# Splitting a layer's weights by DMA: a rounding load for the first part, an accumulating load for the second, both from GpSimd

## The chip, the cores and the metric

The kernel runs on one core of a Trainium2 chip. The metric is device time in microseconds (us) of one execution. The engines are named as in the profile: PE (TensorE matmul), PEld (its weight loads), DVE (VectorE), ACT (ScalarE), POOL (GpSimd) and SP (SyncE, which issues DMAs). An engine's name with a q (SPq, POOLq) is its instruction queue.

## What is computed

One decoder layer in float32 on 512 tokens of width 1024: a token mixer (an SSD group and a retention group behind one input projection), cross attention into 256 memory tokens, and a gated feed-forward with a short convolution, each followed by a layer norm.

```python
mix = _mixer(x, w_in, ..., w_mix_out, ...)      # projections 1024 -> 5648, SSD, retention, 2048 -> 1024
x = _layer_norm(ALPHA * x + mix, ln1_g, ln1_b)
xa = _memory_cross_attention(x, mem, w_xq, w_xk, w_xv, w_xo)
x = _layer_norm(ALPHA * x + xa, ln2_g, ln2_b)
ff = _conv_glu_ffn(x, w_ffn_up, b_ffn_up, ffn_conv_w, ffn_conv_b, w_ffn_down)
x = _layer_norm(ALPHA * x + ff, ln3_g, ln3_b)
```

## The kernel before

All dense products run in float32r, a rounded float32 that PE takes at full rate. To keep float32's precision each operand is split in two float32r parts: a first part h, the operand rounded, and a second part l, what the rounding left. A product is then three matmuls (`mm3`: h by h, h by l, l by h).

The weights come as one stream of 157 groups of [128, 1024] float32 (512 KB each), in the order in which PE uses them; below they are numbered 0 to 156. `Stream.push` fetches the next group and splits it: SP issues a DMA into a raw buffer (line 124), ACT rounds it into `wh` (line 126, a cast), and DVE, or GpSimd for the twelve groups in `POOL_L`, subtracts to get `wl` (line 128). `Stream.get` hands out one group and pushes up to three groups ahead of it: `wh` and `wl` have four buffers each (`RING`), the raw buffers are three (`RAW`). A buffer of `wh` and `wl` is free for group n when PE has finished group n-4.

Groups 0 to 15 are the projections to q, k and v of the retention, 16 to 27 those that feed the convolution, with the retention core woven between, 28 to 43 the two gates, with the SSD core woven between, 44 to 59 the mixer's output projection, 60 to 75 the memory's keys and values, 76 to 91 the attention's query and output projections, and 92 to 156 the feed-forward. A full group is 24 matmuls of 512 columns; for the keys and values it is half as much work. Three places hold four groups at once: the last groups of attention (88 to 91), the first four of the feed-forward (92 to 95, function `halves`), and the very last four (153 to 156, function `last`).

PE's order is the order of writing (`pin`). On the other engines, each of which takes its own instructions in order, a scheduler sets the order. GpSimd's own work is spread over the layer: rotary and SSD products, the reciprocal roots of the norms (lines 257 and 258), and a dozen plain loads of 512 KB that it issues itself: rows of norm weights (line 253), a mask (line 370) and the residual (line 642).

Of the kernel before, what the change touches and what calls it, by code (L numbers as in the profile page):

```python
# [7 lines left out]
F32 = mybir.dt.float32  # L8
# [5 lines left out]
P = 128  # L14
# [15 lines left out]
WARM = 9  # L30
# weight groups whose second part GpSimd takes
POOL_L = set(range(60, 68)) | set(range(92, 96))
RAW = 3
NS = 20

# columns of the constant array
C_ID, C_TRI, C_STR, C_ONE = 0, 128, 256, 384
# [9 lines left out]
C_W = C_SELJ + 4  # L47
# columns of the parameter array
P_CONV, P_GNW, P_GNB, P_FF = 0, 60, 68, 76
# [4 lines left out]
def tile_layer(ctx, tc, wst, wdt, xt, xn, memt, rows, small_row, par, cst, mdec, out):  # L54
    nc = tc.nc
# [3 lines left out]
    ring = ctx.enter_context(tc.tile_pool(name="ring", bufs=RING))  # L59
# [7 lines left out]
    def nm(s):  # L67
        uid[0] += 1
        return f"{s}_{uid[0]}"
# [16 lines left out]
    mult, add, sub = ALU.mult, ALU.add, ALU.subtract  # L86
    tt, stt, ts = nc.vector.tensor_tensor, nc.vector.scalar_tensor_tensor, nc.vector.tensor_scalar
    gtt = nc.gpsimd.tensor_tensor

    def f(t):  # L90
        return t.bitcast(F32)

    # The tensor engine runs its instructions in the order in which they are written here.
    last_pe = [None]
# [14 lines left out]

# [1 line left out]
    class Stream:  # L111
# [6 lines left out]
        def push(self, parts=1, between=None):  # L118
            r = ring.tile([P, 1024], F32, tag="raw", name=nm("raw"), bufs=RAW)
            h = ring.tile([P, 1024], F32R, tag="wh", name=nm("wh"))  # L120
            l = ring.tile([P, 1024], F32R, tag="wl", name=nm("wl"))
            for i in range(parts):
                c = slice(i * 1024 // parts, (i + 1) * 1024 // parts)
                nc.sync.dma_start(out=r[:, c], in_=wst[self.n][:, c])  # L124
                copy = nc.vector.tensor_copy if parts > 1 and i == 0 else nc.scalar.copy
                copy(out=h[:, c], in_=r[:, c])  # L126
                sub_l = gtt if self.n in POOL_L else tt
                sub_l(out=l[:, c], in0=r[:, c], in1=f(h[:, c]), op=sub)  # L128
                if between is not None:
                    between(i, copy)  # L130
            self.q.append((h, l))
            self.n += 1
# [9 lines left out]

    # The tensor engine's clock rises only once it works: it turns over while the first loads are on
    # their way.
    idle = t2(mybir.dt.bfloat16)
# [8 lines left out]

# [1 line left out]
    def mm3(o, a, b, start, stop):  # L156
# [45 lines left out]

# [1 line left out]
    xT = [slot("x", [P, 4, T], F32R) for _ in range(4)]  # L204
# [8 lines left out]
    for j in range(4):  # L213
        r = big([P, 1024])
        rv = r.rearrange("p (k t) -> p k t", k=2)
        xv = xt[j].rearrange("p (k t) -> p k t", k=2)
        h = xT[j // 2][:, 2 * (j % 2):2 * (j % 2) + 2, :]
        l = xT[2 + j // 2][:, 2 * (j % 2):2 * (j % 2) + 2, :]
# [19 lines left out]
    ones = cs[:, C_ONE:C_ONE + P]  # L238
# [26 lines left out]

# [1 line left out]
    QK = [big([P, 2, 512]) for _ in range(NT)]  # L267
# [23 lines left out]

# [1 line left out]
    wdr = cpool.tile([P, KD, 2, 16], F32R, name="wdr")  # L293
# [3 lines left out]
    dt = cpool.tile([P, 64], F32, name="dt")  # L297
# [10 lines left out]
    def dt_chain():  # L308
# [25 lines left out]
        for j in (13, 11, 9, 7, 5, 3, 1):  # L334
# [7 lines left out]
            in0=av.rearrange("p (q j) -> p q j", q=16).unsqueeze(2).to_broadcast([P, 16, 8, 4]),  # L342
            in1=sgn.unsqueeze(1).unsqueeze(3).to_broadcast([P, 16, 8, 4]), op=mult)
# [4 lines left out]
        nc.scalar.activation(out=ev, in_=b[:, :192].rearrange("p (j x) -> p j x", j=3), func=AF.Exp)  # L348
        # The differences of the running sums between two positions come from the tensor engine.
        # Four heads take 32 rows: the sums in two parts against ones, and ones against minus the sums.  # L350
        b = bank()
# [12 lines left out]
    dense = seq(tok(x_lhs, all8, NT, rotary(1)), *[tok(x_lhs, all8, NT, v_done(n)) for n in range(2)])  # L364
    weave(dt_chain(), dense)
    drain(dense)

# [1 line left out]
    maskdec = slot("row", [P, 8, P], F32, 2)  # L369
# [76 lines left out]

# [1 line left out]
    BT = big([P, 2, T])  # L448
# [51 lines left out]
    dense = xbc()  # L500
    weave(retention(), dense)
    drain(dense)

# [1 line left out]
    norm_w = bcast_row(rows[0:1, :])  # L505
# [14 lines left out]
    def ssd():  # L520
# [4 lines left out]
        for c in range(NT):  # L525
# [10 lines left out]
            cb = t2()  # L536
# [4 lines left out]
            def seg(q):  # L541
                g = q // 2
                b = bank()
                r = slice(32 * q, 32 * q + 32)
                mmul(b, seg_w[0][r, 1, tk], sr[r, :])
                # at or before a position the difference is at most 0; the others fall to cb's mask
                es[q] = t2()
                nc.scalar.activation(out=es[q], in_=b, func=AF.Relu, scale=-1.0)
                nc.scalar.activation(out=es[q], in_=es[q], func=AF.Exp, scale=-1.0)
                tt(out=hv(es[q], 4), in0=hv(es[q], 4),  # L550
                   in1=cb[:, g * P:(g + 1) * P].unsqueeze(1).to_broadcast([P, 4, P]), op=mult)
# [46 lines left out]

# [1 line left out]
    def twice_silu(b):  # L600
# [19 lines left out]

# [1 line left out]
    def z_gate(n):  # L622
# [12 lines left out]
    dense = seq(*[feat(xk, T, gate(j)) for j in range(8)], tok(x_lhs, all8, NT, z_gate(0)))  # L635
# [7 lines left out]

# [1 line left out]
    def into_acc(n, scale=None):  # L645
# [31 lines left out]
    dense = seq(*[tok(tok2(yret), all8, NT, into_acc(n, ALPHA)) for n in range(2)])  # L677
# [40 lines left out]
    for j in range(2):  # L718
        r = ring.tile([P, 1024], F32, tag="raw", name=nm("raw"), bufs=RAW)
# [8 lines left out]

# [1 line left out]
    def mk(k):  # L730
# [33 lines left out]

# [1 line left out]
    OT = []  # L766
# [76 lines left out]

    # the last products token by token, each with its norm behind it
    def last(tiles, ks, t, gs, parts=HALVES):
# [25 lines left out]

# [1 line left out]
    lnrow[2] = (bcast_row(rows[5:6, :]), bcast_row(rows[6:7, :]))  # L873
# [13 lines left out]
    half = {}  # L887
# [25 lines left out]
    def halves(i0, n):  # L913
        # the first tiles in two halves of the tokens, while the norm of the other half is under way
        gs = [W.get(8) for _ in range(n)]
        bs = [bank() for _ in range(n)]
        for p in range(2):
            c = slice(256 * p, 256 * p + 256)
            for i in range(n):
                yield from feat(lambda k: (xk(k)[0][:, c], xk(k)[1][:, c]), 256,  # L920
                                lambda o: None, bs[i][:, c], gs[i])
                if p == 1:
                    ff_done(i0 + i)(bs[i])
# [22 lines left out]

# [1 line left out]
def _feat(w, cols):  # L948
# [128 lines left out]
```

## Time and profile before

| | |
|---|---|
| time, median of 2 runs | 956.36 us (955.72 to 956.99) |
| profiled execution, first to last instruction | 953.9 us |
| what lies around it (median less span) | 2.5 us |
| PE busy | 944.3 us, 99% |
| DVE busy | 563.6 us, 59% |
| ACT busy | 340.9 us, 36% |
| POOL busy | 140.0 us, 15% |
| DMA | 95.24 MB, 100 GB/s on average |

The span is the profiled execution's own time from its first to its last instruction; the runs' median is 2.5 us longer. A matmul's end is modelled in the profile, so a busy PE is not PE at its peak, but its idle time is real.

### The profile page before, as it was taken

What the parts mean: (1) busy time and instruction counts of PE and PEld (TensorE: products, weight loads), DVE (VectorE), ACT (ScalarE), POOL (GpSimd) and SP (SyncE); (2) the same over time, 40 slices, a digit from 0 to 9 for tenths busy, and PEclk for the clock granted to TensorE, in tenths of its full rate; (3) what the DMA queues carried; (4) which work ended last, traced back from release to release, by engine and by line L of the source; (5) the groups of instructions that cost most, each with busy time, mean ns of one, the idle gap of its engine ahead of it and who ended that gap; (6) DMA issues with size and microseconds to landing.
All of it is one profiled execution on the core that took longest, in us unless ns stands there. A gap on an engine that the chain in (4) does not pass through costs nothing.

```text
span 953.9 us, 11550 instructions
## 1 busy us (share of the span) xinstructions
PE 944.3 (99%) x4607; PEld 776.5 (81%) x4607; DVE 563.6 (59%) x847; ACT 340.9 (36%) x487; POOL 140.0 (15%) x150
## 2 busy tenths in 40 slices
PE   9999999999999999999999999999999999999996
PEld 6788877788777888889888888988888888888874
DVE  5652566687765463448645668766535566336577
ACT  4122333345443431223533413544323443224420
POOL 1330110014252530065000006000000000000003
PEclk9999999999999999999999999999999999999999
DMA  8233211222211262425621112432322323323202
GB/s 296 87 115 103 67 45 67 67 89 67 67 45 67 89 221 88 154 89 176 221 88 47 67 66 89 136 108 88 98 101 89 111 89 95 103 89 110 89 22 89
DMA packets 26981, 95.24 MB, mean 100 GB/s; under 512 B 3120, under 2 KB 3632, under 8 KB 26928
## 3 DMA queue, kind: packets, MB, share of 16 engines
q1 hardware_dynamic: 25056, 88.09, 27.7%
q0 software_dynamic: 1728, 6.29, 1.9%
q8 instruction: 36, 0.59, 0.3%
q14 instruction: 17, 0.14, 0.1%
q10 hardware_dynamic: 144, 0.13, 0.0%
HBM read 92.41 MB, written 2.10 MB: 99 GB/s over the span
## 4 chain that ended last, share of the span: by engine, by line
PE 97%; DVE 1%; DMA 1%; SPq 0%; issue 0%; ACT 0%; DVEq 0%
PE b L104 95%; PE b L108 3%; DMA raw<-in_wst 1%; DVE acc L699 0%; DVE acc L692 0%; DVE x L153 0%; SPq L221 0%; DVE wl L128 0%; DVE acc L857 0%; DVE st L687 0%; ACT wh L126 0%; SPq L124 0%; DVEq L1073 0%; DVE st L688 0%
## 5 line engine op out<-in xcount | busy, mean ns | idle before, releaser
L104 PE MATMUL b<-x,wh 128*128 128x512 f32 (+1 forms) x1200 | 359.1, 382 | 0.5 <-DVE x L153 0.5
L128 DVE TENSOR_TENSOR wl<-raw,wh 128x1024 fp32r<-128x1024 f32 (+1 forms) x146 | 179.9, 1234 | 225.9 <-ACT wh L126 225.3
L126 ACT CAST wh<-raw 128x1024 fp32r<-128x1024 f32 (+1 forms) x157 | 164.8, 1050 | 311.5 <-PE b L104 275.1
L104 PEld LDWEIGHTS b<-x,wh 128*128 128x128 f32 x1200 | 218.2, 188 | 45.0 <-issue 4.2
L104 PE MATMUL b<-x,wl 128*128 128x512 f32 (+1 forms) x600 | 227.1, 378 | 0.0
L104 PE MATMUL b<-wh,s 128*128 128x512 f32 (+2 forms) x680 | 214.1, 391 | 0.0
L104 PE MATMUL b<-wh,x 128*128 128x512 f32 x512 | 163.2, 395 | 0.0
L104 PEld LDWEIGHTS b<-wh,s 128*128 128x128 f32 (+1 forms) x680 | 127.3, 188 | 30.7 <-issue 5.1
L104 PE MATMUL b<-wl,s 128*128 128x512 f32 (+1 forms) x340 | 131.5, 387 | 0.0
L104 PEld LDWEIGHTS b<-x,wl 128*128 128x128 f32 x600 | 112.9, 188 | 21.3
L104 PEld LDWEIGHTS b<-wh,x 128*128 128x128 f32 x512 | 96.0, 188 | 23.6 <-issue 2.2
L104 PE MATMUL b<-wl,x 128*128 128x512 f32 x256 | 99.9, 390 | 0.7 <-DVE wl L128 0.7
L104 PEld LDWEIGHTS b<-wl,s 128*128 128x128 f32 x340 | 63.9, 188 | 12.2
L257 POOL TENSOR_TENSOR st<-st,epst 128x1 f32<-128x1 f32 (+1 forms) x16 | 3.1, 192 | 479.6 <-DVE st L688 479.2
L894 DVE SCALAR_TENSOR_TENSOR t<-b,pr,t 128x511 f32<-128x511 f32 x86 | 64.1, 746 | 1.4
L104 PEld LDWEIGHTS b<-wl,x 128*128 128x128 f32 x256 | 48.1, 188 | 11.4 <-DVE wl L128 1.1
L128 POOL TENSOR_TENSOR wl<-raw,wh 128x1024 fp32r<-128x1024 f32 x12 | 34.8, 2916 | 68.5 <-ACT wh L126 68.5
L892 ACT ACTIVATE t<-b,cw,pr 128x512 f32<-128x512 f32 x43 | 33.3, 775 | 0.0
L908 ACT CAST s<-t 128x512 fp32r<-128x512 f32 (+1 forms) x22 | 13.6, 620 | 54.3 <-DVE t L906 54.3
L897 ACT ACTIVATE t<-t 128x512 f32<-128x512 f32 x21 | 13.3, 632 | 42.2 <-DVE t L895 42.2
L649 DVE TENSOR_TENSOR acc<-acc,b 128x512 f32<-128x512 f32 x24 | 15.8, 678 | 17.9 <-PE b L104 17.9
L104 PE MATMUL b<-s,wh 128*128 128x256 f32 x128 | 23.4, 285 | 0.0
(166 smaller groups left out, 856.3 us busy)
## 6 DMA issues: line engine op xcount, KB each, us to landing
raw<-in_wst SPq DMA_DIRECT2D x156, 512.0 KB, 3.3
row<-in_rows POOLq DMA_DIRECT2D x7, 512.0 KB, 6.2
acc<-in_xn POOLq DMA_DIRECT2D x4, 512.0 KB, 6.4
s<-in_xt SPq DMA_DIRECT2D x3, 512.0 KB, 7.7
out_y<-acc SPq DMA_DIRECT2D x3, 512.0 KB, 2.6
raw<-in_memt SPq DMA_DIRECT2D x2, 512.0 KB, 3.3
raw<-in_wst SPq DMA_DIRECT2D x2, 256.0 KB, 3.3
s<-in_xt SPq DMA_DIRECT2D x2, 256.0 KB, 4.3
```

Of the source, the lines that this page charges most:

```text
L104: pin(nc.tensor.matmul(o, lhsT=lhsT, rhs=rhs, start=start, stop=stop))
L108: pin(nc.tensor.transpose(o, i, ident[:p, :p]))
L126: copy(out=h[:, c], in_=r[:, c])
L128: sub_l(out=l[:, c], in0=r[:, c], in1=f(h[:, c]), op=sub)
L257: gtt(out=o, in0=v, in1=epst[:, :n], op=add)
L649: tt(out=a, in0=a, in1=b, op=add)
L892: nc.scalar.activation(out=c, in_=u, func=AF.Identity, bias=cw[0][:, i:i + 1], scale=ffp[:, i, 2:3])
L894: stt(out=c[:, d:], in0=u[:, :T - d], scalar=ffp[:, i, 2 - d:3 - d], in1=c[:, d:], op0=mult, op1=add)
L897: nc.scalar.activation(out=c, in_=c, func=AF.Silu)
L908: nc.scalar.copy(out=hd[:n, 0, :], in_=ca[:n, :])
```

## The change

From group 6 on the raw buffer, SP's load and the subtraction are gone. GpSimd issues a DMA straight from the float32 weights into `wh`, whose type is float32r, so that the DMA engines round (line 123 of the changed kernel). ACT then writes minus `wh` into `wl` (line 124), where before it wrote `wh`. GpSimd issues a second DMA of the same weights that adds them onto `wl` (line 125), which leaves the weights less their rounded part. Each group is thus read twice from memory. Groups 0 to 5 keep the old way. RING, and with it the number of groups fetched ahead, stays.

```diff
-POOL_L = set(range(60, 68)) | set(range(92, 96))
+FIRST = 6
...
         def push(self, parts=1, between=None):
-            r = ring.tile([P, 1024], F32, tag="raw", name=nm("raw"), bufs=RAW)
             h = ring.tile([P, 1024], F32R, tag="wh", name=nm("wh"))
             l = ring.tile([P, 1024], F32R, tag="wl", name=nm("wl"))
-            for i in range(parts):
-                c = slice(i * 1024 // parts, (i + 1) * 1024 // parts)
-                nc.sync.dma_start(out=r[:, c], in_=wst[self.n][:, c])
-                copy = nc.vector.tensor_copy if parts > 1 and i == 0 else nc.scalar.copy
-                copy(out=h[:, c], in_=r[:, c])
-                sub_l = gtt if self.n in POOL_L else tt
-                sub_l(out=l[:, c], in0=r[:, c], in1=f(h[:, c]), op=sub)
-                if between is not None:
-                    between(i, copy)
+            if self.n >= FIRST:
+                nc.gpsimd.dma_start(out=h, in_=wst[self.n])
+                nc.scalar.mul(l, f(h), -1.0)
+                nc.gpsimd.dma_start(out=l, in_=wst[self.n], accum_op=add)
+            else:
+                r = ring.tile([P, 1024], F32, tag="raw", name=nm("raw"), bufs=RAW)
...
```

The scheduler places the new DMAs among GpSimd's work. In the feed-forward, groups 96 to 156, GpSimd's queue held nothing for the weights before: two loads of norm rows were followed at once by the last norms.

```order
L253 DMA row_4706<-in_rows 128x1024
L253 DMA row_4708<-in_rows 128x1024
L257 TENSOR_TENSOR st_7130<-st_7129,epst 128x1
L258 TENSOR_TENSOR st_7130<-st_7130,mhalf 128x1
```

Now the same queue, in the middle of the feed-forward, reads as below. A `wh` and the `wl` whose number is one higher are one group, and each `wl` row waits for ACT's multiplication of its group, which waits for that group's `wh` to land.

```order
L123 DMA wh_4982<-in_wst 128x1024
L123 DMA wh_5018<-in_wst 128x1024
L125 DMA wl_4983<-in_wst 128x1024
L125 DMA wl_5019<-in_wst 128x1024
L123 DMA wh_5057<-in_wst 128x1024
L125 DMA wl_5058<-in_wst 128x1024
L123 DMA wh_5093<-in_wst 128x1024
L123 DMA wh_5132<-in_wst 128x1024
L125 DMA wl_5094<-in_wst 128x1024
L125 DMA wl_5133<-in_wst 128x1024
```

Three groups take turns: two go out as a pair of first loads and a pair of second loads, the third goes out alone, with its second load straight behind its first.

In the memory's keys and values GpSimd's queue in the changed kernel is one group further ahead: the first load of a group stands before the second load of the group in front of it, all the way from group 62 to 79.

```order
L125 DMA wl_3476<-in_wst 128x1024
L123 DMA wh_3540<-in_wst 128x1024
L125 DMA wl_3524<-in_wst 128x1024
L123 DMA wh_3557<-in_wst 128x1024
L125 DMA wl_3541<-in_wst 128x1024
L123 DMA wh_3574<-in_wst 128x1024
```

On ACT in the feed-forward the cast's place is taken by the multiplication (L124), between the same neighbours as before: the bias of one tile (L897), its SiLU (L902) and the rounding of the hidden tile (L913).

```order
L913 CAST s_5054<-t_760_5012 128x512
L124 ACTIVATE wl_5058<-wh_5057 128x1024
L897 ACTIVATE t_769_5087<-b_5062,cw_4621,pr 128x512
L902 ACTIVATE t_769_5087<-t_769_5087 128x512
L124 ACTIVATE wl_5094<-wh_5093 128x1024
```

What moved is the source of the row's wait: the cast waited for a raw buffer that SP had filled ahead of time, the multiplication waits for a load that GpSimd issues only when a buffer of `wh` comes free.

## Rows read from the trace of the kernel before

**Rows 1.** The page's part 1: busy time, share of the span, instructions.

```profile
span 953.9 us, 11550 instructions
PE 944.3 (99%) x4607; PEld 776.5 (81%) x4607; DVE 563.6 (59%) x847; ACT 340.9 (36%) x487; POOL 140.0 (15%) x150
```

**Rows 2.** The page's part 4, the chain that ended last, by engine.

```profile
PE 97%; DVE 1%; DMA 1%; SPq 0%; issue 0%; ACT 0%; DVEq 0%
```

**Rows 3.** The page's part 5: the split's groups, busy, mean ns, idle before.

```profile
L128 DVE TENSOR_TENSOR wl<-raw,wh 128x1024 fp32r<-128x1024 f32 (+1 forms) x146 | 179.9, 1234 | 225.9 <-ACT wh L126 225.3
L126 ACT CAST wh<-raw 128x1024 fp32r<-128x1024 f32 (+1 forms) x157 | 164.8, 1050 | 311.5 <-PE b L104 275.1
L128 POOL TENSOR_TENSOR wl<-raw,wh 128x1024 fp32r<-128x1024 f32 x12 | 34.8, 2916 | 68.5 <-ACT wh L126 68.5
```

**Rows 4.** Line 126 by stretches: stretch, length, DVE, ACT busy (casts), clock, DMA.

```profile
23.30:83.60 60.30, 0.00 (x0) 10.54 (x10) 1.00 0.32 103
83.60:180.70 97.10, 0.00 (x0) 12.61 (x12) 1.00 0.20 67
180.70:318.50 137.80, 0.00 (x0) 16.78 (x16) 1.00 0.19 63
318.50:424.90 106.40, 0.00 (x0) 21.02 (x20) 1.00 0.40 137
424.90:475.60 50.70, 0.00 (x0) 16.73 (x16) 1.00 0.58 191
475.60:567.30 91.70, 0.00 (x0) 12.68 (x12) 1.00 0.22 73
602.30:922.30 320.00, 0.00 (x0) 64.32 (x61) 1.00 0.29 96
```

**Rows 5.** POOL's instructions in order of time, 338 to 356: start, length, what.

```profile
342.02 2.20 POOL L642 DMA_DIRECT2D acc<-in_xn  x4
344.21 1.04 POOL L253 DMA_DIRECT2D row<-in_rows  x2
```

**Rows 6.** DMA issues alone, at 342.1, 342.7, 344.9, 445.2: KB, us to landing.

```profile
acc<-in_xn POOLq DMA_DIRECT2D x1, 512.0 KB, 3.6
...
acc<-in_xn POOLq DMA_DIRECT2D x1, 512.0 KB, 4.4
...
row<-in_rows POOLq DMA_DIRECT2D x1, 512.0 KB, 12.1
...
row<-in_rows POOLq DMA_DIRECT2D x1, 512.0 KB, 7.7
```

**Rows 7.** The page's part 6: DMA issues, KB each, median us to landing.

```profile
raw<-in_wst SPq DMA_DIRECT2D x156, 512.0 KB, 3.3
row<-in_rows POOLq DMA_DIRECT2D x7, 512.0 KB, 6.2
```

**Rows 8.** POOL's groups by line, DMA instructions: busy, mean ns, idle before.

```profile
L253 POOL DMA_DIRECT2D row<-in_rows x7 | 3.9, 565 | 1.1 <-DVE acc L699 1.1
...
L370 POOL DMA_DIRECT2D row<-in_mdec x1 | 0.8, 769 | 0.0
```

**Rows 9.** DVE's instructions in order of time from 341.5: start, length, what.

```profile
342.06 0.75 DVE L632 SCALAR_TENSOR_TENSOR s<-s,st,row 128x512 f32<-128x512 f32 x1 [0.77 <-POOL st L631]
342.73 1.22 DVE L128 TENSOR_TENSOR wl<-raw,wh 128x1024 fp32r<-128x1024 f32 x1
```

**Rows 10.** Stretches: length, PE, PEld, DVE, ACT, POOL busy, clock, DMA.

```profile
181.00:319.00 138.00, 138.00 (x650) 107.28 (x649) 92.76 (x138) 59.88 (x98) 44.17 (x37) 1.00 0.19 64
11.50:12.30 0.80, 0.14 (x1) 0.00 (x0) 0.79 (x1) 0.79 (x1) 0.00 (x0) 1.00 1.04 425
948.00:954.00 6.00, 0.00 (x0) 0.00 (x0) 2.80 (x5) 0.00 (x0) 1.01 (x2) 0.72 0.44 165
```

More of the change, by code (lines that the diff above doesn't have):

```diff
@@ L118, in push @@
         def push(self, parts=1, between=None):
-            r = ring.tile([P, 1024], F32, tag="raw", name=nm("raw"), bufs=RAW)
             h = ring.tile([P, 1024], F32R, tag="wh", name=nm("wh"))
             l = ring.tile([P, 1024], F32R, tag="wl", name=nm("wl"))
-            for i in range(parts):
-                c = slice(i * 1024 // parts, (i + 1) * 1024 // parts)
-                nc.sync.dma_start(out=r[:, c], in_=wst[self.n][:, c])
-                copy = nc.vector.tensor_copy if parts > 1 and i == 0 else nc.scalar.copy
-                copy(out=h[:, c], in_=r[:, c])
-                sub_l = gtt if self.n in POOL_L else tt
-                sub_l(out=l[:, c], in0=r[:, c], in1=f(h[:, c]), op=sub)
-                if between is not None:
-                    between(i, copy)
+            if self.n >= FIRST:
[4 more added lines that the diff above has]
+                r = ring.tile([P, 1024], F32, tag="raw", name=nm("raw"), bufs=RAW)
+                for i in range(parts):
+                    c = slice(i * 1024 // parts, (i + 1) * 1024 // parts)
+                    nc.sync.dma_start(out=r[:, c], in_=wst[self.n][:, c])
+                    copy = nc.vector.tensor_copy if parts > 1 and i == 0 else nc.scalar.copy
+                    copy(out=h[:, c], in_=r[:, c])
+                    tt(out=l[:, c], in0=r[:, c], in1=f(h[:, c]), op=sub)
+                    if between is not None:
+                        between(i, copy)
             self.q.append((h, l))
```

## The prediction

> **What bounds the kernel now.** I read the busy times first, then the chain of work that ended last. PE is busy for 944.3 of 953.9 us [rows 1], and the chain that ended last runs on PE for 97%, on DVE for 1% and on a DMA for 1% [rows 2]. So no change to the split can gain more than the 9.6 us in which PE is idle; being 19.1 us faster, which is 2% and about what a measurement of this kernel can tell from no change, is out of reach. The question is whether the weights keep PE supplied. The rows of the split show why they do now: ACT's 157 casts waited mostly on PE, that is on a free buffer, and hardly on data [rows 3]. SP's loads land 3.3 us after issue [rows 7] in raw buffers that are filled ahead of the free buffer, so from a buffer coming free to a split group it is a cast and a subtraction, 1.05 + 1.23 = 2.3 us [rows 3]. The pace is read from the casts by stretch [rows 4]: 320.0 us for 61 groups in the feed-forward, 50.7 us for 16 of keys and values, 8.1 and 8.6 us a group where the retention and SSD cores are woven in.
>
> **What goes.** Of DVE's 146 subtractions seven, of the first six groups, stay; 139 of 1.23 us leave (171 us) and GpSimd's twelve of 2.9 us too (35 us) [rows 3]. DVE holds 1% of the chain, so this is worth at most 9 us and I take nothing: PE's matmuls already cover that work. SP's loads go, and with them the raw buffers, which were the only place where data could wait for a buffer. ACT keeps one instruction a group; I take the multiplication at the cast's 1.05 us.
>
> **What comes: rounds on GpSimd's queue.** GpSimd takes its instructions in order. Where a group's second load stands straight behind its first, the queue stands still until the first load has landed and ACT has multiplied; behind that waits the next group's first load, and PE waits for that group. One such round takes a landing, a multiplication and an issue. The multiplication is 1.05 us. An issue took 0.57 us on average and 0.77 us at most [rows 8]; the second load names two things to read, so I take 0.77.
>
> The landing is the term that decides. Every first load now stands right behind the second load of the group before on the same queue. The nearest row is the second DMA of a train of six, at 342.65 us right behind a plain load: 4.4 us [rows 5, 6]. That is the lower end, for an accumulating load that costs what a plain one does. Such a load must also read what it adds to. If that read costs as much as another load, the first load behind it lands one step later. A step is read from the same train: its first DMA landed at 345.6 us and its sixth at 344.7 + 12.1 = 356.8, so (356.8 - 345.6) / 5 = 2.2 us [rows 5, 6], and the upper end is 6.6 us. I take 6.2 us, the median of the seven loads of norm rows [rows 7], near the upper end since adding needs that read. For the range I go down to 4.4 and up to 7.7 us, the second of a pair at 445.1 us [rows 6]. A round is then 6.2 + 1.05 + 0.77 = 8.0 us, between 6.2 and 9.5.
>
> The row of 4.4 us holds no accumulating load, so it can't say whether the read counts. The Trainium skill ("Collectives: The Full Stack", The bandwidth ceiling) states that a reduce step runs at half the rate of a copy, because each output needs two reads on the same queue side. No run here shows it yet; by it the landing is the upper end, 6.6 us, a round 8.4 us and the time 1090, and without it 4.4, 6.2 and 968 us.
>
> **The rounds against PE's pace.** The order of GpSimd's queue in the changed kernel says how many rounds a stretch has. Where two first loads go out together, as with two groups of three in the feed-forward, the second costs a step of 2.2 us and no round. Where the first load is one group ahead throughout (groups 62 to 79), a round carries two groups. Against the stretches of [rows 4]:
> Groups 6 to 15: 8 rounds and 2 steps, 68.4 us against 60.3, so 8.1 lost. Groups 16 to 27: 11 and 1, 90.2 against 97.1, nothing lost, since PE has the retention's work. Groups 28 to 43: 15 and 1, 122.2; GpSimd's own SSD work of 44.2 us [rows 10] stands in the same queue, and half of it, an estimate, falls into waits; 144.3 against 137.8, 6.5 lost. Groups 44 to 63: 14 and 6, 125.2 against 106.4, 18.8 lost. Groups 64 to 79: 8 rounds for 16 groups, 64.0 against 50.7, 13.3 lost; the DMA engines were already at 0.58 there, 29 us, so two loads a group need 59 us and three loads' worth 88. Groups 80 to 91: 11 and 1, 90.2 against 91.7, nothing. Groups 96 to 156: 5 groups at half a round, 37 rounds and 19 steps, 357.8 against 325 (60 periods in 320 us, and one more), 32.8 lost. The sum is 79.5 us.
>
> **Restarts.** Where four groups are held at once (88 to 91, 92 to 95, 153 to 156) nothing can be fetched ahead, and PE needs a new group soon after a buffer comes free. That was 2.3 us away; now it is landing, multiplication, issue and landing, 6.2 + 1.05 + 0.77 + 6.2 = 14.2. The difference of 11.9 us is halved, an estimate, for what PE still has to do: 6 us, three times 18 (0 to 36).
>
> **Sum.** 953.9 + 79.5 + 18 = 1051.4 us of span, and 2.5 us around it, as the median has now: 1054 us, 10% above 956.36. With rounds of 9.5 us the seven stretches lose 20, 10, 29, 40, 25, 15 and 92 us, and with 30 for restarts the time is about 1220.
>
> **DVE and the descriptors.** GpSimd's DMA instructions at 342.02 to 344.2 us took 0.55 us on average while DVE ran two operations on two SBUF inputs, one of 1.22 us [rows 5, 9]. The Trainium skill ("SBUF — State Buffer", SBUF: two separate sides) says that GpSimd can't write descriptors while DVE holds the port that they share, and so speaks against a queue of loads on GpSimd beside a busy DVE. By it those issues would have been stretched and each round would be up to one DVE operation longer, some 0.75 us and 1125 us in all; the row speaks against it, and the change takes 171 us off DVE besides. Its time lies within the range.
>
> **Rivals.** First, not slower: the accumulating load costs no more than a plain one. Then the landing is 4.4 us, a round 6.2, and every stretch of [rows 4] fits (the tightest: 49.6 against 50.7 for keys and values, 100 against 106.4 in groups 44 to 63); restarts of 4 us leave 968 us. It decides from rounds of some 6.3 us on downward. For it: SP's loads land in 3.3 us, and SP's traffic, which stood in the way of the 6.2 us rows, is gone. Against it: the read of the destination.
> Second, both loads are slow: rounding in the DMA engine costs a second pass as well. Then the landing is 6.6 + 2.2 = 8.8 us, a round 10.6, the stretches lose 348 us, restarts 24, and the time is some 1330. No row has a rounding DMA; nothing speaks against it but that bytes in and out are the same.
> Third, PE's clock. It is granted in full in every stretch of work, and a wait of 0.7 us at 11.5 us did not lower it; in the last 6 us, after PE's last matmul, it averages 0.72, so it does fall when PE is idle for some microseconds [rows 10]. Waits of about 2 us a round are between the two. If it were at half for a third of the 482 us of the feed-forward and groups 44 to 79, PE's work there would take 160 us more, a part of it inside waits that are there anyway: about 1180.
>
> **How the numbers follow.** My forecast, rounds of 7 to 9.5 us, has 0.56 (985 to 1220); the plain-cost rival 0.20; slow loads 0.13; the clock 0.06; the rest 0.05, half of it above 1240. Predicted is 1054 us. The range 960 to 1240 holds the forecast, the first rival and the clock, 0.82. Within 2% is the first rival, 0.2, and little else; faster by over 2% is excluded by PE's busy time but for a mistake in it, 0.01; slower 0.79.
>
> **What would show it.** Right: PE idle some 10% of the span, its waits ended by the second part's DMA (`wl`); GpSimd's queue waiting for ACT, ACT for the DMA of `wh`; landings of `wh` near 6.2 us; ACT's multiplications 8.0 us apart in lone rounds; the retention stretch no longer than now. Wrong: landings near 4.4 us and PE still at 99%, landings above 8 us, or GpSimd's DMA instructions of several microseconds, which would make the issue and not the landing the longest part of a round.

## The result, and the profile after

The changed kernel takes 1151.46 us (median of 2 runs, 1149.92 to 1153.0) against 956.36: the ratio is 1.204, with a 95% interval of 1.1997 to 1.2082. It was predicted to be slower, at 1054 us in a range of 960 to 1240. The direction and the mechanism held; the loss, 195 us, is twice the 98 that the terms added up to.

Part 1 and part 4 of the page after, to be read against [rows 1, 2]:

```profile
span 1148.2 us, 11595 instructions
PE 1007.4 (88%) x4607; PEld 805.7 (70%) x4607; DVE 404.3 (35%) x708; ACT 338.1 (29%) x487; POOL 318.3 (28%) x440
...
PE 30%; issue 30%; DMA 22%; POOL 10%; ACT 4%; DVE 2%; SPq 0%; POOLq 0%; ACTq 0%; DVEq 0%
```

DVE is relieved, as the change meant, from 563.6 to 404.3 us. But the chain, 97% PE before, is now 30% PE; DMAs hold 22%, GpSimd's instructions 10%, ACT 4%, and 30% is "issue", pauses for which the chain names nothing that was waited for. PE stands idle for 1148.2 - 1007.4 = 140.8 us, where it had 9.6. That is 131 of the 194 us by which the span grew; the other 63 are PE's own busy time, which rose from 944.3 with the same 4607 instructions.

The split's groups in part 5 (busy, mean ns of one, idle before) and its loads in part 6 (median us to landing), against [rows 3, 7]:

```profile
L124 ACT ACTIVATE wl<-wh 128x1024 fp32r<-128x1024 f32 x151 | 159.8, 1058 | 546.0 <-DMA wh<-in_wst 466.1
L125 POOL DMA_DIRECT2D wl<-in_wst x151 | 132.0, 874 | 677.2 <-ACT wl L124 609.4
...
L123 POOL DMA_DIRECT2D wh<-in_wst x151 | 113.4, 793 | 56.4 <-PE b L104 54.2
...
q0 software_dynamic: 45216, 164.65, 61.7%
...
wh<-in_wst POOLq DMA_DIRECT2D x151, 512.0 KB, 6.3
wl<-in_wst POOLq DMA_DIRECT2D x151, 512.0 KB, 5.4
```

This is the ring of waits that the prediction spoke of: GpSimd's second load waits for ACT's multiplication (609.4 us), the multiplication for the first load (466.1), and the first load, which should wait for a free buffer from PE, hardly does (54.2): when its turn comes on the queue, the buffer has long been free. Before, ACT's cast waited on PE for 275.1 us, a sign of weights ready too early. Who waits for the second part is in the list of waits (us in total, times, longest):

```profile
PE b L104 <- DMA wl<-in_wst: 107.3, 54, 6.0
```

The stretches of [rows 4], cut at the same multiplications as the casts were there, for all engines (PE, PEld, DVE, ACT, POOL busy, granted clock, DMA share, GB/s). The sixth runs from group 80 to the first of the feed-forward, 92, and the seventh over the four groups of `halves`:

```profile
28.12:99.67 71.55, 68.04 (x298) 53.65 (x297) 19.03 (x45) 12.98 (x17) 25.37 (x36) 0.98 0.65 147
99.67:205.83 106.16, 95.48 (x531) 76.61 (x530) 44.09 (x115) 35.96 (x58) 27.95 (x40) 0.97 0.55 124
205.83:363.60 157.77, 150.99 (x668) 116.38 (x669) 84.97 (x123) 59.93 (x98) 67.58 (x72) 0.95 0.49 110
363.60:500.77 137.17, 115.19 (x506) 93.89 (x505) 34.72 (x52) 30.72 (x42) 45.26 (x69) 0.93 0.71 174
500.77:580.73 79.96, 63.57 (x332) 52.76 (x331) 13.46 (x20) 25.09 (x32) 24.57 (x36) 0.95 0.97 233
580.73:695.99 115.26, 102.94 (x497) 85.12 (x496) 49.99 (x96) 33.48 (x70) 21.70 (x31) 0.94 0.49 108
695.99:727.53 31.54, 23.05 (x177) 22.57 (x176) 8.95 (x14) 8.81 (x11) 6.91 (x11) 0.89 0.65 159
727.53:1110.95 383.42, 337.73 (x1418) 269.75 (x1416) 112.63 (x196) 118.72 (x148) 84.45 (x119) 0.96 0.70 163
```

| groups | before, us | after | lost | predicted |
|---|---|---|---|---|
| 6 to 15 | 60.3 | 71.6 | 11.3 | 8.1 |
| 16 to 27 | 97.1 | 106.2 | 9.1 | 0 |
| 28 to 43 | 137.8 | 157.8 | 20.0 | 6.5 |
| 44 to 63 | 106.4 | 137.2 | 30.8 | 18.8 |
| 64 to 79 | 50.7 | 80.0 | 29.3 | 13.3 |
| 80 to 95, with two restarts | 126.7 | 146.8 | 20.1 | 12 |
| 96 to 156 | 320.0 | 383.4 | 63.4 | 32.8 |
| after that, with the third | 31.6 | 37.3 | 5.7 | 6 |

(126.7 is 602.3 - 475.6 from the marks of [rows 4].) The start adds 4.8 us. Every stretch lost more than predicted but the last, and the table gives the experiments their places.

How a turn of the queue looks, in GpSimd's order of time in the feed-forward (start, length; in brackets the idle time before and what ended it):

```profile
897.79 0.86 POOL L125 DMA_DIRECT2D wl<-in_wst  x1 [0.75 <-ACT wl L124]
898.34 0.87 POOL L123 DMA_DIRECT2D wh<-in_wst  x1
906.72 0.85 POOL L125 DMA_DIRECT2D wl<-in_wst  x1 [7.51 <-ACT wl L124]
907.26 1.42 POOL L123 DMA_DIRECT2D wh<-in_wst  x2
915.26 0.87 POOL L125 DMA_DIRECT2D wl<-in_wst  x1 [6.58 <-ACT wl L124]
919.51 0.86 POOL L125 DMA_DIRECT2D wl<-in_wst  x1 [3.38 <-ACT wl L124]
920.06 0.87 POOL L123 DMA_DIRECT2D wh<-in_wst  x1
```

From the lone first load at 898.34 to the pair at 907.26 is one round of 8.9 us, from there to 920.06 a round of 12.8 us that carries two groups. Between the issues the queue does nothing. Taken from the starts of the first loads from group 101 on in this trace, where one and two groups take turns regularly, 18 rounds of one group took 8.82 us on average and 18 of two groups 10.80, so three groups take 19.6 us. PE needed three times 320.0 / 60 = 5.33, that is 16.0 us, before.

### The profile page after: what moved, and what is told of

The parts are those of the page before. It is cut to its first block, busy times and chain, and to the rows that moved or that the text cites. A ratio compares the mean times of both kernels' runs of the same rounds, so it can differ in the third digit from the quotient of the medians.

```text
span 1148.2 us, 11595 instructions
## 1 busy us (share of the span) xinstructions
PE 1007.4 (88%) x4607; PEld 805.7 (70%) x4607; DVE 404.3 (35%) x708; ACT 338.1 (29%) x487; POOL 318.3 (28%) x440
## 3 DMA queue, kind: packets, MB, share of 16 engines
q0 software_dynamic: 45216, 164.65, 61.7%
## 4 chain that ended last, share of the span: by engine, by line
PE 30%; issue 30%; DMA 22%; POOL 10%; ACT 4%; DVE 2%; SPq 0%; POOLq 0%; ACTq 0%; DVEq 0%
PE b L104 29%; DMA wh<-in_wst 16%; DMA wl<-in_wst 5%; POOL wh L123 4%; POOL wl L125 4%; ACT wl L124 3%; POOL s L631 1%; DMA row<-in_mdec 1%; DMA raw<-in_wst 1%; DVE t L899 1%; PE b L108 1%; POOL st L635 1%; ACT t L897 0%; DVE t L555 0%; POOL row L258 0%
## 5 line engine op out<-in xcount | busy, mean ns | idle before, releaser
L104 PE MATMUL b<-x,wh 128*128 128x512 f32 (+1 forms) x1200 | 370.5, 393 | 0.0
L124 ACT ACTIVATE wl<-wh 128x1024 fp32r<-128x1024 f32 x151 | 159.8, 1058 | 546.0 <-DMA wh<-in_wst 466.1
L125 POOL DMA_DIRECT2D wl<-in_wst x151 | 132.0, 874 | 677.2 <-ACT wl L124 609.4
L104 PE MATMUL b<-wh,s 128*128 128x512 f32 (+2 forms) x680 | 225.3, 408 | 0.0
L104 PE MATMUL b<-wl,s 128*128 128x512 f32 (+1 forms) x340 | 140.8, 414 | 49.5 <-DMA wl<-in_wst 49.3
L899 DVE SCALAR_TENSOR_TENSOR t<-b,pr,t 128x511 f32<-128x511 f32 (+1 forms) x86 | 64.2, 749 | 189.6 <-ACT t L897 188.2
L123 POOL DMA_DIRECT2D wh<-in_wst x151 | 113.4, 793 | 56.4 <-PE b L104 54.2
L158 DVE TENSOR_TENSOR s<-b,s 128x512 fp32r<-128x512 f32 x24 | 16.1, 686 | 79.1 <-ACT s L157 79.1
L656 DVE SCALAR_TENSOR_TENSOR acc<-acc,b 128x512 f32<-128x512 f32 x24 | 16.3, 685 | 61.0 <-PE b L104 61.0
L897 ACT ACTIVATE t<-b,cw,pr 128x512 f32<-128x512 f32 x43 | 32.7, 764 | 9.3 <-PE b L104 9.3
L104 PE MATMUL b<-s,wl 128*128 128x256 f32 x64 | 20.8, 325 | 9.7 <-DMA wl<-in_wst 9.7
```

Source lines behind the costliest of these rows:

```text
L104: pin(nc.tensor.matmul(o, lhsT=lhsT, rhs=rhs, start=start, stop=stop))
L123: nc.gpsimd.dma_start(out=h, in_=wst[self.n])
L124: nc.scalar.mul(l, f(h), -1.0)
L125: nc.gpsimd.dma_start(out=l, in_=wst[self.n], accum_op=add)
L158: tt(out=l, in0=src, in1=f(h), op=sub)
L656: stt(out=a, in0=a, scalar=scale, in1=b, op0=mult, op1=add)
```

## The experiments

Each was timed against the kernel before, which took 956.2 to 956.7 us beside them. Where stretches are given, they are measured between the first matmuls on a group's weights, and groups 96 to 156 (the feed-forward) to the end of the span, so that all kernels are cut at the same work. By this measure groups 96 to 156 take 343.0 us in the kernel before and 416.5 in the changed one.

**Is it the adding, or the order?** Two kernels take away one each, and a third both. The first leaves `accum_op` out:

```diff
-                nc.gpsimd.dma_start(out=l, in_=wst[self.n], accum_op=add)
+                nc.gpsimd.dma_start(out=l, in_=wst[self.n])
```

> Leaves the adding out: the second load overwrites its buffer, so the second part is the rounded weights again and the output is not the layer's. The number, size, order and waits of all loads stay. Theory of rounds (GpSimd's queue stands still from a first load's issue to ACT's multiplication, and the adding lengthens the landing of the load behind it): the first loads land some 4.4 us after issue in place of 6.3, a lone round falls from 8 to 9 us to about 6.5, and the time to 1030 to 1060 us. Rival, the rounding is what is slow: landings and time stay, 1130 us or more.

1016.23 us, ratio 1.0625 [1.0608, 1.0643]: below what I expected. (The trace is of the shortest of its five executions, 1006.01 us.) Its groups on GpSimd and its landings:

```profile
L123 POOL DMA_DIRECT2D wh<-in_wst x151 | 82.2, 545 | 92.2 <-PE b L104 89.3 <-DVE t L340 1.6 <-issue 0.9
L125 POOL DMA_DIRECT2D wl<-in_wst x151 | 81.5, 540 | 542.6 <-ACT wl L124 509.1 <-issue 17.8 <-ACT s L448 5.5
...
wh<-in_wst POOLq DMA_DIRECT2D x151, 512.0 KB, 4.7
wl<-in_wst POOLq DMA_DIRECT2D x151, 512.0 KB, 3.8
```

GpSimd still waits for ACT for 509.1 us, with the same order on its queue, yet 135 of the 195 us are gone. A first load behind a plain second one lands after 4.7 us instead of 6.3; the rounds of one and of two groups in the feed-forward fall to 7.19 and 9.28 us, 16.5 for three groups, close to PE's 16.0. So the wait is harmless as long as a round is short enough: it is the landing behind an adding load that lifts the round over PE's pace.

The second kernel keeps the adding and moves each second load on the queue behind the next group's first load, so that no first load stands behind a wait for its own predecessor's multiplication:

```diff
-                nc.gpsimd.dma_start(out=h, in_=wst[self.n])
+                first = nc.gpsimd.dma_start(out=h, in_=wst[self.n])
                 nc.scalar.mul(l, f(h), -1.0)
-                nc.gpsimd.dma_start(out=l, in_=wst[self.n], accum_op=add)
+                self.late.append((l, self.n))
+                self.second(first, 1 if self.n not in (91, 95, self.total - 1) else 0)
```

(`late` holds the second loads back, and `second` issues those that are due behind `first`; at groups 91, 95 and 156 nothing is held back.)

> Same loads, same bytes, but on GpSimd's queue each group's second load stands behind the first load of the next group, throughout (as in groups 62 to 79 of the changed kernel). Theory of rounds: a round carries two groups, the feed-forward returns to about 5.4 us a group, the keys and values stay near 5.0 us a group where the DMA engines are busy, and the time is 990 to 1030 us. Rival, the DMA engines are the bound (two loads a group, one of them adding, whatever the order): no more than 20 us better than 1151, so 1130 or more.

1039.73 us, ratio 1.0868 [1.0843, 1.0893], a little above the theory's range and far from the rival's. Its waits, and a window in the keys and values:

```profile
POOL wh L132 <- PE b L104: 437.6, 115, 13.4
...
POOL wl L122 <- ACT wl L133: 129.3, 75, 6.8
...
430.00:500.00 70.00, 55.50 (x332) 47.96 (x331) 25.30 (x36) 22.00 (x29) 25.48 (x38) 0.98 0.96 220
```

GpSimd now waits on PE for a free buffer, as ACT's casts did before, and 609.4 us of waiting for ACT are 129.3. With the same two loads a group and the same adding, 112 us are back. What is left has other places: 23.8 us in groups 60 to 75, where the DMA engines are at 0.96, 19.8 in groups 96 to 156, 9.5 in groups 28 to 43, 14.6 and 11.1 around the places that hold four groups (76 to 91 and 92 to 95).

The third takes both away, and the fourth keeps the adding and the late order, with a fifth buffer of `wh` and `wl` (and one raw buffer instead of three).

> The late second load, and a plain one: it overwrites instead of adding, so wl holds the weights and not the rest, and the output is not the layer's. By the theory this takes the adding's traffic out of a queue that no longer waits for ACT: 960 to 985 us, and the memory's keys and values lose under 10 us where the adding version lost 24. If the adding itself were cheap and only the order counted, the time would stay near the late version's 1040 us (1025 or more).

1003.14 us, ratio 1.0497 [1.0474, 1.052]: the keys and values lose 6.9 us, as expected, but the time is 18 us over the range, since groups 28 to 43 lose 11.1, groups 96 to 156 12.7 and groups 76 to 95 14.1 even so. Adding thus costs 37 us in the late order (1039.73 - 1003.14) and 135 in the changed kernel's (1151.46 - 1016.23); the order costs 112 us with the adding and 13 without it. So most of the loss is neither alone but their product, a slow landing inside a queue that waits for it. With neither, 47 us are still lost (1003.14 - 956.47), in the stretches just named, the 6.0 us of groups 44 to 59 and the keys and values; what makes them up was not tested.

> The late second load (each behind the next group's first load) with five buffers. By the theory two separate things are then gone, the queue's wait for ACT and the wait for a free buffer that took its place (437.6 us of GpSimd's waits in the late version, most of it harmless); what stays is what the DMA engines can't carry in the memory's keys and values (24 us lost there with four buffers) and the restarts (some 10): 985 to 1020 us. By the rival, in which the adding loads fill the DMA engines all along, the depth changes nothing: 1030 us or more.

1013.73 us, ratio 1.0595 [1.0577, 1.0613], inside the range. Groups 96 to 156 lose 5.8 us instead of 19.8, while the keys and values still lose 21.4: depth cures a late buffer, not full DMA engines.

**Does depth help without the order?** Five buffers alone:

```diff
-RING = 4
+RING = 5
...
-RAW = 3
+RAW = 1
```

> Five buffers of wh and wl instead of four, so one group more is fetched ahead (the raw buffers of the first groups are cut to one to make room). By the rounds theory GpSimd's queue still takes one or two groups per round, a round is as long as before, and a deeper ring only fills once: 1110 to 1150 us. By the rival (a free buffer comes too late for a load of 6 us, a multiplication and a load of 5 us in a row) one more group's 5 us of cover hides most of it: under 1050 us.

1151.67 us, ratio 1.2042 [1.2005, 1.2079], no change. The rival, a buffer that comes free too late, falls as the main cause. The scheduler changed GpSimd's order here too, and stretches moved both ways (groups 16 to 27 are 11.6 us longer than in the changed kernel, groups 44 to 59 7.7 shorter), so the total alone says little; but where the same turns of one and two groups stand, in groups 96 to 156, the time is 418.9 us against 416.5. A queue that delivers a group per round is not helped by more room behind it.

**How many groups a round carries.** Here the queue's order is set by hand over the whole stream, with the same loads and the same adding (`inline` puts a DMA behind the one written before it). First each group alone:

```diff
-                nc.gpsimd.dma_start(out=h, in_=wst[self.n])
+                self.inline(nc.gpsimd.dma_start(out=h, in_=wst[self.n]))
                 nc.scalar.mul(l, f(h), -1.0)
-                nc.gpsimd.dma_start(out=l, in_=wst[self.n], accum_op=add)
+                self.late[self.n] = l
+                for k in [self.n]:
+                    self.inline(nc.gpsimd.dma_start(out=self.late[k], in_=wst[k], accum_op=add))
```

> The same loads, multiplication and number of instructions; only their order on GpSimd's queue is set by hand: every second load straight behind its own first load, from group 6 to 156, so that each round carries one group. In the feed-forward of the changed kernel a round of one group measured 8.8 us and one of two 10.8. By the rounds theory the feed-forward takes 61 x 8.8 = 537 us instead of 416, the keys and values 141 instead of 76, groups 44 to 59 141 instead of 117, and groups 16 to 43, where nearly all were alone already, stay: 1360 us (1300 to 1400). By the rival, in which the traffic of the adding loads sets the time, fewer loads lie side by side and it is no slower than 1160 us.

1381.56 us, ratio 1.4447 [1.4418, 1.4476], as the theory reckoned and 220 us from the rival's bound. GpSimd's order of time:

```profile
938.43 0.86 POOL L132 DMA_DIRECT2D wh<-in_wst  x1
946.41 0.86 POOL L136 DMA_DIRECT2D wl<-in_wst  x1 [7.11 <-ACT wl L133]
946.96 0.86 POOL L132 DMA_DIRECT2D wh<-in_wst  x1
```

This round is 8.5 us, and the average of 60 is 8.19, the prediction's 8.0. Groups 60 to 75, which the changed kernel took in 76.0 us with its order one group ahead, need 130.4: the same bytes, only in turn.

Then pairs:

```diff
-                for k in [self.n]:
+                for k in ([self.n - 1, self.n] if self.n % 2 else [self.n] if self.n == self.total - 1 else []):
```

> The same loads again, in pairs throughout: two first loads, then their two second loads. By the rounds theory a round of two groups of 10.8 us is 5.4 us per group, just under what PE takes for a group in the feed-forward (5.6): it falls from 416 to some 350 us; groups 16 to 43 lose 4 us instead of 30, groups 44 to 59 fall from 117 to some 95, groups 76 to 91 by 10, and the keys and values, where the order was better than pairs, lose 10: 1040 us (1010 to 1080). By the rival, that the adding's traffic or a late buffer for the second group of a pair is what counts, 1110 us or more.

1090.62 us, ratio 1.1403 [1.1384, 1.1422]: 61 us better than the changed kernel, but 10 us over the range. Groups 6 to 27 are at 164.3 us, against 162.7 before; but the feed-forward fell to 399.4 us only, where 350 was expected, and groups 28 to 43 lost 19.4 us, more than the 15.2 of the changed kernel; why they did was not tested. (The trace is of the longest of its five executions, 1103.05 us, so these stretches are on the long side.) GpSimd's order of time, and ACT's:

```profile
910.62 1.41 POOL L132 DMA_DIRECT2D wh<-in_wst  x2
917.99 0.87 POOL L136 DMA_DIRECT2D wl<-in_wst  x1 [5.97 <-ACT wl L133]
922.63 0.86 POOL L136 DMA_DIRECT2D wl<-in_wst  x1 [3.77 <-ACT wl L133]
923.18 1.40 POOL L132 DMA_DIRECT2D wh<-in_wst  x2
...
916.63 1.06 ACT L133 ACTIVATE wl<-wh 128x1024 fp32r<-128x1024 f32 x1 [3.84 <-DMA wh<-in_wst]
917.60 0.76 ACT L908 ACTIVATE t<-b,cw,pr 128x512 f32<-128x512 f32 x1
920.75 0.62 ACT L924 CAST s<-t 128x512 fp32r<-128x512 f32 x1 [2.39 <-DVE t L922]
921.28 1.05 ACT L133 ACTIVATE wl<-wh 128x1024 fp32r<-128x1024 f32 x1
```

The second multiplication of the pair stands on ACT behind the rounding of a hidden tile, which waits 2.39 us for DVE. The two second loads are 4.6 us apart, and a round is 12.6 us here and 12.04 on average of 30. A second in-order queue has entered the round.

**ACT's queue.** The first test of it moved the negation to DVE in the changed kernel and let the scheduler set the order.

```diff
-                nc.scalar.mul(l, f(h), -1.0)
+                nc.vector.tensor_scalar(out=l, in0=f(h), scalar1=-1.0, scalar2=None, op0=mult)
```

> The negation moves from ACT to DVE; nothing else. If the rounds on GpSimd's queue cost what they cost because the multiplication stands in ACT's queue (1.06 us each, and in the feed-forward behind the bias and the SiLU, which makes the second group of a pair cost 4.2 us where 2.2 was reckoned), then each turn of three groups there gets some 2.5 us shorter, 20 turns give back 50 us, and the rest of the layer some 25: 1075 us (1050 to 1110). If the length of the round is the load's landing and the traffic of the adding loads alone, the queue of ACT is not the cause and the time stays at 1130 or more.

1154.96 us, ratio 1.208 [1.2062, 1.2098], which looked like the rival. But the scheduler had also changed GpSimd's order. The rounds were shorter, 8.00 and 10.52 us, and fewer of them carried two groups: 14 pairs and 28 single groups in the regular turns (from group 100 on), against 18 and 18. The two effects cancel, so the run told nothing of the cause. The test was repeated with the changed kernel's order written down, then with pairs:

> The negation on DVE again, with GpSimd's queue held in the very order of the changed kernel, since without that the queue had 14 pairs among 56 groups of the feed-forward instead of 18 among 54. There the rounds measured 8.0 and 10.5 us against 8.8 and 10.8 with ACT. By the rounds theory 18 turns of three groups get 1.1 us shorter each: 20 us in the feed-forward, 5 in groups 44 to 59 and some 8 in groups 16 to 43: 1115 us (1095 to 1130). By the rival, in which the negation's place plays no part, 1145 us or more.

1119.61 us, ratio 1.172 [1.1674, 1.1765], as expected: 32 us come from moving the negation to DVE, where it also takes 0.69 us instead of 1.06. Groups 96 to 156 fall by 22 us (416.5 to 394.3), with rounds of 8.19 and 10.30 us.

> The pairs throughout, with the negation on DVE instead of ACT and the same order of GpSimd's queue. In the pairs with ACT a round in the feed-forward measured 12.0 us, where 10.8 was expected: the multiplication of the second group stood on ACT behind a cast of the hidden tile that waited 2.4 us for DVE, and the second loads of a pair were 4.6 us apart. If that is what made the pairs miss, a round falls to the 10.3 us that pairs with DVE measured in the changed kernel's order, the feed-forward from 399 to some 355 us and the whole to 1050 us (1035 to 1065). If the missing time is due to buffers that come late for the second group or to the adding loads, it stays at 1080 us or more.

1065.95 us, ratio 1.1141 [1.1109, 1.1173], 1 us outside the range. The feed-forward is at 359.1 us as expected, and GpSimd's first load waits for a buffer again:

```profile
914.39 0.55 POOL L132 DMA_DIRECT2D wh<-in_wst  x1 [3.72 <-PE b L104]
916.99 0.89 POOL L136 DMA_DIRECT2D wl<-in_wst  x1 [2.05 <-DVE wl L133]
918.86 0.90 POOL L136 DMA_DIRECT2D wl<-in_wst  x1 [0.98 <-DVE wl L133]
```

The rounds there last 10.75 us, twice PE's pace of 5.33. What spoils the sum is groups 60 to 75, 92.6 us against 80.2 with ACT, and there one negation above all. That of group 63 starts 9.3 us after its load has landed, behind the first layer norm's work on DVE (the last row below; the first is group 62's):

```profile
451.07 0.69 DVE L133 TENSOR_SCALAR wl<-wh 128x1024 fp32r<-128x1024 f32 x1 [4.16 <-DMA wh<-in_wst]
...
462.68 0.64 DVE L133 TENSOR_SCALAR wl<-wh 128x1024 fp32r<-128x1024 f32 x1
```

Its round takes 20.8 us. The other seven rounds of these groups take 9.1 to 12.3 us, as with ACT (9.9 to 12.0).

**What each kind of load costs.** One kernel gives SP the first load and ACT the rounding, so that only the adding load is on GpSimd; the other keeps the rounding load on GpSimd, loads a raw copy by SP and subtracts on DVE.

```diff
-                nc.gpsimd.dma_start(out=h, in_=wst[self.n])
-                nc.scalar.mul(l, f(h), -1.0)
+                r = ring.tile([P, 1024], F32, tag="raw", name=nm("raw"), bufs=RAW)
+                nc.sync.dma_start(out=r, in_=wst[self.n])
+                nc.scalar.copy(out=h, in_=r)
+                nc.vector.tensor_scalar(out=l, in0=f(h), scalar1=-1.0, scalar2=None, op0=mult)
```

> The first part goes the old way (SP loads into the raw buffers, ACT rounds), DVE writes its negative, and only the accumulating load stays on GpSimd. Two loads a group and the adding stay. Theory of rounds: no first load stands behind a wait any more, the feed-forward runs at PE's pace, keys and values keep about 25 us of loss to the DMA engines, 965 to 1000 us. Rival, the accumulating load is itself too slow or too late for PE: 1080 us or more.

992.64 us, ratio 1.0376 [1.0361, 1.0392], inside the range. GpSimd's queue again waits for long, now for DVE, and it costs nothing in groups 6 to 59, since no first load stands behind that wait:

```profile
POOL wl L127 <- DVE wl L126: 543.3, 123, 11.6
```

More than half of what is lost, 18.8 us, falls in groups 60 to 75.

```diff
+                r = ring.tile([P, 1024], F32, tag="raw", name=nm("raw"), bufs=RAW)
+                nc.sync.dma_start(out=r, in_=wst[self.n])
                 nc.gpsimd.dma_start(out=h, in_=wst[self.n])
-                nc.scalar.mul(l, f(h), -1.0)
-                nc.gpsimd.dma_start(out=l, in_=wst[self.n], accum_op=add)
+                tt(out=l, in0=r, in1=f(h), op=sub)
```

> The rounding load on GpSimd stays, the second part goes the old way: SP loads the raw weights and DVE subtracts. Two loads a group, none adds, and GpSimd's queue never waits for ACT. Theory of rounds: rounding in the DMA engines costs nothing, 956 to 970 us. Rival, loads issued by GpSimd or rounded on the way are slow in themselves: 1000 us or more.

976.53 us, ratio 1.021 [1.0194, 1.0227], 7 us above the range. Rounding in the DMA costs little more than a plain load, if anything: the two loads of the same group land nearly alike, though on different queues.

```profile
raw<-in_wst SPq DMA_DIRECT2D x156, 512.0 KB, 4.0
wh<-in_wst POOLq DMA_DIRECT2D x151, 512.0 KB, 4.2
```

No version beats the kernel before. At 99% PE busy there was nothing to gain, and the best of them still doubles the weights' traffic.

## Why the prediction was right, and where its size was not

**Right: the mechanism.** The rounds are there as described, with the landing that was taken (6.2 us; 6.3 measured) and the lone round that followed from it (8.0; 8.19 on average when all rounds are lone, in groups 96 to 156: landing 6.08, wait for ACT 0.15, multiplication 1.06, the two handoffs 0.34 and 0.57). That the landing came out so close is partly luck: 6.2 was the median of plain loads among other traffic, taken because it lay near the upper end. PE idles 12% of the span, and the second part's DMA ends its waits. Forcing all rounds single added 230 us, forcing them into pairs took 61 away, and the late order 112, all with the same loads. That cause is shown, not argued.

**Right: an adding load costs a second pass.** Of the three rivals the first (968 us) is the kernel with a plain second load. It landed at 4.7 us against the 4.4 taken, and its time was 1016; its rounds of two and one group fit PE's pace, as that rival said, but the keys and values (8.1 us), the restarts (8.2 and 6.4) and groups 96 to 156 (15.6) still lost. The queue's occupancy gives the price: q0 took 61.7% of 1148.2 us, 708 us of all 16 engines, and in the plain kernel 51.7% of 1004.2, 519 us. The difference is 189 us for 151 adding loads, 1.25 us each. A load that doesn't add takes 519 / 314 = 1.65 (two for each of 151 groups, which round, and the dozen of [rows 5, 8]), so an adding one takes 2.90, or 1.76 times as long. Two other pairs of kernels give more: 3.20 against 1.63 us, 1.96 times, from the late order with and without adding (72.0% of 1040.1 us and 50.9% of 1005.5), and 3.04 against 1.65, 1.84 times, from the adding load alone and the rounding load alone on GpSimd (48.4% of 990.1 and 27.6% of 975.0 us, with the dozen plain loads in both). Why the three differ was not tested. The Trainium skill ("Collectives: The Full Stack", The bandwidth ceiling) puts a collective's reduce step at half the rate of a copy; the runs agree nearly, with 1.76 to 1.96. By it the landing was 6.6 and the time 1090, closer to the result than my 1054 was.

**Mis-sized: the rounds of the feed-forward.** A turn of three groups was put at 8.0 + 8.0 + 2.2 = 18.2 us and took 8.82 + 10.80 = 19.6; 18 turns make 25 of the 30.6 us that this stretch lost beyond the forecast. The step of 2.2 was right (10.80 - 8.82 = 2.0). The lone round was not: in those 18 rounds the landing was 6.81 us on average, behind two adding loads instead of one, the wait for ACT 0.04, the multiplication 1.06, from its end to the second load 0.36 and from there to the next first load 0.55, which is 8.82. The handoffs are 0.91 instead of the one issue of 0.77, and the landing 0.6 longer. I had taken one landing for every place of the queue, though the pair before it doubles what is ahead of a load.

**Missed: ACT's own queue.** The multiplication was put at 1.05 us with no wait before it. Alone in its round it began 0.04 us after the landing; as the second of a pair it began 1.21 us after it in the changed kernel and 2.35 in the kernel of pairs (means from group 101 on). Moving the negation to DVE gave back 32 us in the same order, and in pairs 25 (1090.62 - 1065.95). In the changed kernel little of that is ACT's queue: a turn of three groups fell from 19.62 to 18.49 us, of which two shorter operations (0.69 us on DVE for 1.06) make 0.74 and a shorter landing in the lone round 0.31. In pairs the second loads of a round came 2.7 us apart instead of 3.8, and there the queue is the larger part.

**Missed: stretches added up as a whole.** "Groups 16 to 27 [...] 90.2 against 97.1, nothing lost" compared two sums. PE's pace in that stretch is uneven, as ACT's casts of groups 22 to 26 in the trace of the kernel before show (start, length, idle before):

```profile
123.56 1.05 ACT L126 CAST wh<-raw 128x1024 fp32r<-128x1024 f32 x1
137.70 1.05 ACT L126 CAST wh<-raw 128x1024 fp32r<-128x1024 f32 x1 [8.40 <-PE b L104]
144.06 1.05 ACT L126 CAST wh<-raw 128x1024 fp32r<-128x1024 f32 x1 [3.68 <-PE b L104]
151.32 1.04 ACT L126 CAST wh<-raw 128x1024 fp32r<-128x1024 f32 x1 [0.82 <-PE b L104]
165.84 1.05 ACT L126 CAST wh<-raw 128x1024 fp32r<-128x1024 f32 x1 [8.33 <-PE b L104]
```

The gaps are 14.1, 6.4, 7.3 and 14.5 us. A round of 8 us loses against the short ones and can't win it back in the long ones, when the ring is full and the queue waits for a buffer. Had each gap been raised to 8.0 the stretch would have come out some 12 us longer; 9.1 were lost. With a plain second load, and so shorter rounds, the stretch lost 0.6 us, with single rounds throughout 22.0. That the retention stretch would be no longer than now was one of the prediction's own signs of being right, and it failed. The same holds for groups 28 to 43, where gaps of 5.4 to 7.2 stand between those of 8 to 13. There GpSimd's own SSD work comes in too: 4.8 to 11.1 us were lost in the kernels with a plain second load, with late ones and with the rounding load alone, whose first loads are all on GpSimd, and none with the first loads on SP. That this work in the queue is the reason is argued from the places, not tested.

**Mis-sized: the keys and values.** Eight rounds of 8.0 us for 16 groups gave 64.0; 80.0 were taken. The rounds are not the bound there: the DMA engines are at 0.97 in the window above. Sixteen groups at 1.65 + 2.90 us are 73 us of all engines, and at 1.63 + 3.20 us 77. The prediction had that bound in its hand, "three loads' worth 88", and took the smaller number, though the larger of two bounds is the one that holds.

**Restarts** were put at 18 us; the last one measured 5.7, and groups 80 to 95 with the other two lost 20.1 against 12.

**The clock.** The third rival, a fall of PE's clock, came in beside the forecast rather than instead of it. Stretches of the changed kernel around one wait (columns as above):

```profile
914.00:918.00 4.00, 4.00 (x19) 3.07 (x17) 1.57 (x3) 1.99 (x3) 0.87 (x1) 1.00 0.36 41
918.00:921.40 3.40, 0.85 (x4) 0.65 (x4) 1.45 (x3) 1.88 (x3) 1.41 (x2) 1.00 0.71 128
921.40:924.80 3.40, 3.40 (x9) 2.65 (x9) 1.50 (x4) 0.62 (x1) 0.00 (x0) 0.50 0.93 207
```

After PE had waited 2.55 us for `wl`, the clock stood at 0.50, which is 1.2 of 2.4 GHz, and PE started 9 matmuls in that row where the pace of the first row gives 16. With a mean of 0.949 over the span, (1 - 0.949) x 1148.2 = 59 us of full clock were not granted, 48 of them while PE was busy; that is most of the 63 us by which its busy time grew. Not all of it is loss: where the queue sets the time, a slower PE only waits less. With single rounds the clock was lowest, 0.898, and the feed-forward still went at 8.19 us a group. Of the 40 us that groups 6 to 43 lost, PE's idle time is 21.0 (the length less PE's busy time in the first three stretches above), and at the clock of those rows some 13 us of full clock are missing. How much of the 40 a full clock would have given back stays open; no run held it apart.

**GpSimd's descriptors.** The prediction set a rule of the Trainium skill ("SBUF — State Buffer", SBUF: two separate sides) aside, by which GpSimd can't write descriptors while DVE holds the port that they share. The runs bear that out as far as they go: GpSimd's loads took 540 and 545 ns each in the kernel with a plain second load, with DVE busy 400.8 us, 546 in the one with the rounding load alone, with 577.7, and 874 and 793 in the changed one, with 404.3. It is the adding that lengthens them, not DVE's work; no run here shows the wait that the rule speaks of. The section speaks of DVE operations in a two-port mode, and no trace tells an operation's mode, so the two operations of [rows 9] were a weaker test of it than the prediction took them for.

## What to carry to other kernels

Before a load moves to another engine's queue, write down what stands ahead of it there and what that waits for. A load that waits for a result of an earlier load turns a stream into rounds, one landing, one operation and the handoffs each, and the number of groups that a round carries then matters as much as what the loads cost: 1382, 1151, 1091 and 1040 us here, for the same transfers, and 1016 in the order of the 1151 without the adding. Compare such a round with each gap of the consumer and not with a stretch's mean, and where two bounds apply take the larger. When one edit lets a scheduler move others, fix the order before the edit is judged.

## What the runs showed of the hardware

- A DMA that rounds float32 to float32r on the way costs nearly what a plain one does: 4.2 us to landing beside 4.0 for the plain load of the same group (the one on GpSimd's queue, the other on SP's), and 3.5 us for the first load at 202.1 us in the changed kernel, with nothing ahead of it.
- A DMA that adds to its destination takes 1.76 to 1.96 times as long on the engines (2.90 against 1.65 us of all 16 here, 3.20 against 1.63 in the late order), lands after 5.4 us where the plain one took 3.8, and its instruction on GpSimd is recorded with 874 ns against 540. What stands right behind it starts 0.54 us after it, so the recorded length is not the time for which the queue is held.
- From the end of ACT's multiplication to the start of the load that waits for it, 0.36 us passed.
